# One product for gate and up, half of down in three float32r products, the last two blocks placed on chip

## The chip, the cores and the metric

The kernel runs on one core of a Trainium2 chip. The metric is the device time of one execution in microseconds (us), as the median of the runs.

## The reference

One layer of a diffusion backbone: 512 latent tokens of width 1024, 256 context tokens, one batch. First a token-mixing part (retention and gated DeltaNet in both directions, merged through one output projection), then a mixture of experts. The change touches the second part only. For each token a router takes 8 of 64 experts with weights, and

```
routed[t] = sum over the 8 experts e of  wts[t,e] * ( (silu(x[t] @ w_gate[e]) * (x[t] @ w_up[e])) @ w_down[e] )
shared[t] = (silu(x[t] @ w_sh_gate) * (x[t] @ w_sh_up)) @ w_sh_down
out[t]    = x1[t] + modulated rmsnorm(routed[t] + shared[t])
```

in float32, with `w_gate`, `w_up` 1024x256 and `w_down` 256x1024 for each expert. `x1` is the stream after the first part.

## The kernel before, in words

Everything up to about 700 us is the token-mixing part; it stays as it is. `phaseO` ends it: it writes `x1` into the output tensor (`self.out`), the normed tokens `h2` with the 64 routing weights beside them into DRAM (`h2d`, 1088 columns), and starts two sums in DRAM, `accd[0]` with the shared expert's result and `accd[1]` with zeros.

`phaseM` is the loop `for e in range(NE + 2)` (L1424), one block of up to 128 tokens for each expert (`NE` = 64), and one more, block 64, for an expert with more tokens than fit. For still more there is a loop on the chip (`tc.For_i`, L1459) behind it, whose count is read at run time. Iteration `e` works on three blocks at once: the products with gate and up of block `e`, the down product of block `e - 1`, and the transposed tokens of block `e + 2`.

* `prepare(e)` (L1284): GpSimd gathers the block's token rows from `h2d` with an indirect DMA into one of six buffers `xg`. The routing weight `W[e]` is a column of that buffer.
* `make(e, part)` / `turn` (L1232): TensorE transposes half of the tokens, ScalarE casts them to float32r (`h`), VectorE subtracts to get the remainder (`l`). A float32 product is then three float32r products, `h*h + h*l + l*h`: `mm3`, L111 to L113.
* `load(e, n)` (L1185): SyncE's queue loads one weight matrix of 1 MB; `n` is 0, 1, 2 for gate, up, down. Gate and up go into six buffers (`GU`, those called `w` and `wgu` in the profile), down into three (`DW`, called `wd`). For block 64 GpSimd does it, by an index.
* `convert(e, n)` (L1277): `conv` splits a gate or up matrix into cast (ScalarE, L1171) and remainder (VectorE, L1173), in two of seven buffers that all conversions share, and then issues the load of three blocks later into the buffer just read.
* `proj` (L1241): 8 x 3 products of 256 columns for gate, and the same for up, into two halves of one PSUM tile. `act` takes silu and the product, `turn_act` transposes it (`aT`).
* `down` (L1261): `aT` times the raw down weight as a plain float32 product, 2 halves of 512 columns x 2 parts of the contraction; in the trace each such product is two matmul instructions. The two halves are scaled by `W[e]` on VectorE and ScalarE into `y`, and GpSimd adds `y` to the sum in DRAM with an indirect DMA (L1272). Even and odd blocks go to different sums, the last four all to `accd[1]`.

After the loop, four tiles of 128 tokens are finished (L1473 on): `accd[1]` is loaded and added to `accd[0]` (loaded earlier), the norm's factor is formed with a power on GpSimd, the result is scaled, and `x1` is added, for two tiles by a DMA that adds in DRAM, for two on VectorE.

Each engine works through its instructions in order. The order is the scheduler's: it starts from the program's, lets instructions that it thinks are ready go ahead, and obeys `issue_after`. A wait at the head of an engine's queue holds up all behind it.

## Time and profile before

| | us |
|---|---|
| median of 3 runs (lowest, highest) | 1408.96 (1408.09, 1412.23) |
| the profiled execution | 1415.91 |
| its span, first to last instruction | 1414.1 |
| PE (TensorE matmul) busy | 1324.8 |
| DVE (VectorE) busy | 906.7 |
| ACT (ScalarE) busy | 653.4 |
| POOL (GpSimd) busy | 409.6 |
| HBM read, written | 326.59 MB, 48.31 MB |

The busy times are sums over the whole span and mix stages with different limits; what counts for this change is the loop over experts, from about 712 us, and the end behind it, from about 1381. Matmuls are pipelined, so a matmul's listed duration is longer than the step from one to the next. "Idle before, releaser" in a row is the engine's idle time ahead of these instructions and what ended it.

### The profile page before, as it was taken

Reading aid. Unit: us, or ns where it says so; the run is one execution under the profiler, and the core shown is the slowest. Engines: PE = TensorE matmul, PEld = TensorE weight load, DVE = VectorE, ACT = ScalarE, POOL = GpSimd, SP = SyncE. Lnnn points to the kernel's source line nnn. Section 1 sums busy time; section 2 is a strip of 40 time slices with the busy share of each in tenths; the row PEclk is TensorE's granted clock in tenths of the full one; section 3 lists DMA queues with packets and bytes.
Section 4 is the critical chain, followed back from the end, with each engine's and each line's share of the span. In section 5 each row is a group of like instructions: output and inputs, shape, how many; then the busy total and the mean of one; then the engine's idle time right before and its main releaser. Section 6 shows DMA issues by size and latency. Waiting matters only on the chain.

```text
span 1414.1 us, 20716 instructions
## 1 busy us (share of the span) xinstructions
PE 1324.8 (94%) x7848; PEld 1074.7 (76%) x7848; DVE 906.7 (64%) x1270; ACT 653.4 (46%) x926; POOL 409.6 (29%) x330
## 2 busy tenths in 40 slices
PE   6999988899999999999999999999999999999990
PEld 1678866798787777778888787878788888878770
DVE  5645796457676555547668666666666666666543
ACT  5533432553333222334355555555656565555531
POOL 0315544865321000003222222222222222224312
PEclk9899998999999999999999999999999999999995
DMA  7554411102316577575699999999999999999954
GB/s 275 181 141 117 121 56 35 52 16 74 88 49 179 178 214 223 152 259 195 249 386 349 352 370 345 373 351 364 362 366 361 368 364 361 367 364 338 326 183 127
DMA packets 137817, 340.51 MB, mean 241 GB/s; under 512 B 28218, under 2 KB 83038, under 8 KB 112756
## 3 DMA queue, kind: packets, MB, share of 16 engines
q1 hardware_dynamic: 110952, 289.46, 57.2%
q0 software_dynamic: 19584, 38.99, 10.9%
q10 hardware_dynamic: 7180, 10.72, 2.2%
q8 instruction: 63, 1.03, 0.3%
q14 instruction: 38, 0.31, 0.1%
HBM read 326.59 MB, written 48.31 MB: 265 GB/s over the span
## 4 chain that ended last, share of the span: by engine, by line
PE 43%; DMA 7%; issue 1%; ACT 1%; POOL 1%; DVE 0%; DVEq 0%; SPq 0%; ACTq 0%; POOLq 0%
PE cs L1267 13%; PE acc L111 7%; PE acc L113 7%; PE acc L112 7%; DMA w<-in_w_up_dram 4%; PE ci L1236 3%; DMA w<-in_w_gate_dram 2%; PE ci L1066 2%; PE acc L1078 1%; PE acc L1256 1%; DMA w<-acc 1%; POOL fr L127 0%; DMA acc<-y,slots 0%; DMA acc<-y,sl_i 0%; ACT wh L1171 0%
## 5 line engine op out<-in xcount | busy, mean ns | idle before, releaser
L111 PE MATMUL acc<-wh,xT 128*128 128x256 f32 x1040 | 302.2, 291 | 0.0
L113 PE MATMUL acc<-wh,xT 128*128 128x256 f32 x1040 | 291.0, 280 | 0.0
L112 PE MATMUL acc<-wl,xT 128*128 128x256 f32 x1040 | 290.6, 279 | 0.0
L1173 DVE TENSOR_TENSOR wl<-w,wh 128x2048 fp32r<-128x2048 f32 x88 | 201.5, 2291 | 76.2 <-PE acc L112 75.2
L1267 PE MATMUL cs<-wd,aT 128*128 128x512 f32 x520 | 234.6, 594 | 4.5 <-DMA wd<-in_w_down_dram 3.6
L1272 POOL DMA_INDIRECT acc<-y,slots x64 | 101.9, 1593 | 466.5 <-ACT y L1269 427.8
L1171 ACT CAST wh<-w 128x2048 fp32r<-128x2048 f32 x88 | 167.5, 1904 | 99.5 <-PE acc L113 70.2
L111 PEld LDWEIGHTS acc<-wh,xT 128*128 128x128 f32 x1040 | 196.6, 189 | 0.2 <-issue 0.2
L112 PEld LDWEIGHTS acc<-wl,xT 128*128 128x128 f32 x1040 | 196.1, 189 | 0.2 <-issue 0.2
L113 PEld LDWEIGHTS acc<-wh,xT 128*128 128x128 f32 x1040 | 195.5, 188 | 0.0
L1267 PEld LDWEIGHTS cs<-wd,aT 128*128 128x128 f32 x520 | 93.8, 190 | 99.0 <-issue 95.1
L1239 DVE TENSOR_TENSOR xT<-ci,xT 128x512 fp32r<-128x512 f32 x130 | 89.2, 687 | 96.5 <-ACT xT L1238 96.1
L100 ACT CAST wu<-raw 128x1024 fp32r<-128x1024 f32 (+1 forms) x73 | 75.1, 1036 | 104.6 <-DMA raw<-in_w_in_dram 68.0
L111 PE MATMUL acc<-hTx,wu 128*128 128x512 f32 (+1 forms) x296 | 119.6, 404 | 1.5 <-ACT wu L100 1.5
L113 PE MATMUL acc<-hTx,wu 128*128 128x512 f32 (+1 forms) x296 | 117.7, 398 | 1.5 <-DVE wu L107 1.5
L1173 DVE TENSOR_TENSOR wl<-wgu,wh 128x2048 fp32r<-128x2048 f32 x42 | 96.2, 2291 | 34.6 <-PE acc L112 34.4
L112 PE MATMUL acc<-hLx,wu 128*128 128x512 f32 (+1 forms) x296 | 117.1, 396 | 0.0
L107 DVE TENSOR_TENSOR wu<-raw,wu 128x1024 fp32r<-128x1024 f32 (+1 forms) x61 | 78.7, 1299 | 55.4 <-ACT wu L100 55.4
L1171 ACT CAST wh<-wgu 128x2048 fp32r<-128x2048 f32 x42 | 79.8, 1901 | 53.5 <-PE acc L113 35.5
L1236 PEld LDWEIGHTS ci<-ident,xg 128*128 128x128 f32 x520 | 72.5, 191 | 30.6 <-issue 30.2
L1228 POOL DMA_INDIRECT xg<-h2d,slots x64 | 75.5, 1180 | 35.6 <-issue 18.0
L1236 PE MATMUL ci<-ident,xg 128*128 128x128 f32 x520 | 78.7, 275 | 0.1
(493 smaller groups left out, 2374.3 us busy)
## 6 DMA issues: line engine op xcount, KB each, us to landing
wd<-in_w_down_dram SPq DMA_DIRECT2D x64, 1024.0 KB
w<-in_w_gate_dram SPq DMA_DIRECT2D x43, 1024.0 KB
w<-in_w_up_dram SPq DMA_DIRECT2D x43, 1024.0 KB
raw<-in_w_in_dram SPq DMA_DIRECT2D x56, 512.0 KB
wgu<-in_w_gate_dram SPq DMA_DIRECT2D x21, 1024.0 KB
wgu<-in_w_up_dram SPq DMA_DIRECT2D x21, 1024.0 KB
mraw<-in_w_mod_dram SPq DMA_DIRECT2D x32, 512.0 KB
wm<-in_w_mod_dram SPq DMA_DIRECT2D x16, 512.0 KB
```

The costliest lines, as they stand in the source:

```text
L100: nc.scalar.copy(dst, src)
L107: (self.nc.gpsimd if eng == "pool" else self.nc.vector).tensor_tensor(dst, src, hi.bitcast(F32), op=OP.subtract)
L111: mm(out, ah, bh, start=start, stop=False)
L112: mm(out, ah, bl, start=False, stop=False)
L113: mm(out, al, bh, start=False, stop=stop)
L1171: nc.scalar.copy(h[:, i:i + max(n, 1024)], w[:, i:i + max(n, 1024)])
L1173: eng(l[:, i:i + n], w[:, i:i + n], h[:, i:i + n].bitcast(F32), op=OP.subtract)
L1228: nc.gpsimd.indirect_dma_start(xg[:, :], None, self.h2d[:, :], bass.IndirectOffsetOnAxis(ap=ix, axis=0), bounds_check=511, oob_is_err=False)
L1236: nc.tensor.transpose(ps[:, k * 128:k * 128 + 128], xv[:, :, c * 4 + k], self.ident)
L1239: tt(l, ps, h.bitcast(F32), op=OP.subtract)
L1267: nc.tensor.matmul(ps, aT[:, m], wd[:, s], start=k == 0, stop=k == 1)
L1272: nc.gpsimd.indirect_dma_start(self.accd[acc][:, :], bass.IndirectOffsetOnAxis(ap=sx, axis=0), y[:, :], None, bounds_check=511, oob_is_err ...
```

## The change

* Gate and up of a block are converted into one pair of tiles, `GH[e % 2]` and `GL[e % 2]`, and `proj` takes both in one product of 512 columns (two pieces of 256). It runs in two parts, four of eight contraction steps ahead of `turn_act` and four behind it. ScalarE casts each matrix in two pieces of 1024 columns.
* Half of the down weight (the first 512 of 1024 columns) is split too, into `DP` (one buffer), and the activations into `aP`; this half of the down product is `mm3`, the other stays plain float32. `convert(e, 2)` stands at the end of iteration `e`.
* `xg` has three buffers in place of six, and the routing weight is copied out of it (`wcol`). One remainder tile lies where three of the six were. The first loads are in another order.
* The results of blocks 63 and 64 are not added in DRAM. `down_parts` leaves them on chip as cast and remainder, `places` writes one-hot matrices of the rows' tokens, and `finish` multiplies the two, so that a PSUM tile holds what they add to 128 tokens. The sums in DRAM are loaded earlier (`accd[1]` in iteration 63, `accd[0]` in 64), `x1` in iteration 62, all four tiles of it.
* `finish` stands in the program ahead of the loop for further blocks, and once more in its body.

```diff
+        GU = [wp.tile([128, 2048], F32, name=f"wgu{i}") for i in range(4)]
+        GH = [wp.tile([128, 2, 2048], F32R, name=f"gh{i}") for i in range(2)]
+        GL = [wp.tile([128, 2, 2048], F32R, name="gl0"), self.hxpool.tile([128, 2, 2048], F32R, name="gl1", tag="b1")]
+        DP = wp.tile([128, 2, 2, 512], F32R, name="wdp")
...
+        def convert(e, n):
+            if e > NE:
+                return
+            w = raw(e, n)
+            if n < 2:
+                h, l = GH[e % 2][:, n], GL[e % 2][:, n]
+                for i in (0, 1024):
+                    nc.scalar.copy(h[:, i:i + 1024], w[:, i:i + 1024])
+            else:
+                h, l, w = DP[:, 0], DP[:, 1], w.rearrange("p (k f) -> p k f", k=2)[:, :, 0:512]
+                nc.scalar.copy(h, w)
+            tt(l, w, h.bitcast(F32), op=OP.subtract)
+            if n < 2:
+                load(e + 3, n)
...
-        for e, n in ((0, 0), (0, 1), (1, 0), (0, 2), (1, 1), (2, 0), (1, 2), (2, 1), (2, 2)):
+        for e, n in ((0, 0), (0, 1), (1, 0), (1, 1), (0, 2), (1, 2), (2, 0), (2, 1), (2, 2)):
...
-        xg6, xg3 = q.tile([128, 3, 1088], F32, name="xg", bufs=1), self.hxpool.tile([128, 3, 1088], F32, name="xg", tag="b1")
-        xgs = [x[:, i] for x in (xg6, xg3) for i in range(3)]
+        xg3 = q.tile([128, 3, 1088], F32, name="xg", bufs=1)
+        xgs = [xg3[:, i] for i in range(3)]
...
-        def proj(out, x, w, first=True):
-            for k in range(8):
+        def proj(out, x, e, ks=range(8)):
+            o = out.rearrange("p (n f) -> p n f", n=2)
+            for k in ks:
                 s = slice(k * 256, k * 256 + 256)
-                self.mm3(out, x[0][:, k], x[1][:, k], w[0][:, s], w[1][:, s], k == 0, k == 7)
+                self.mm3(o, x[0][:, k], x[1][:, k], GH[e % 2][:, :, s], GL[e % 2][:, :, s], k == 0, k == 7)
...
-            aT = q.tile([128, 256], F32, name="aT")
+            aT, aP = q.tile([128, 256], F32, name="aT"), q.tile([128, 2, 256], F32R, name="aP", bufs=1)
+            nc.scalar.copy(aP[:, 0], ps[:, 0:256])
+            tt(aP[:, 1], ps[:, 0:256], aP[:, 0].bitcast(F32), op=OP.subtract)
             nc.scalar.copy(aT, ps[:, 0:256])
-            return aT
+            return aT, aP
+        def down_half(aT, wd, c):
+            ps = self.pc()
+            for k in range(2):
+                m = slice(k * 128, k * 128 + 128)
+                if c == 0:
+                    self.mm3(ps, aT[1][:, 0, m], aT[1][:, 1, m], DP[:, 0, k], DP[:, 1, k], k == 0, k == 1)
+                else:
+                    nc.tensor.matmul(ps, aT[0][:, m], wd[:, k * 1024 + 512:k * 1024 + 1024], start=k == 0, stop=k == 1)
+            return ps
...
+        def down_parts(aT, ws, wd, y):
+            for c in range(2):
+                ps = down_half(aT, wd, c)
+                h, l = y[:, c * 512:c * 512 + 512], y[:, 1024 + c * 512:1536 + c * 512]
+                nc.scalar.activation(h, ps, AF.Copy, scale=ws)
+                self.parted = nc.vector.scalar_tensor_tensor(l, ps, ws, h.bitcast(F32), op0=OP.mult, op1=OP.subtract)
+            return y
+        def places(oh, row):
+            at = q.tile([128, 4], F32, name="at", bufs=2)
+            for t in range(4):
+                ts(at[:, t:t + 1], row, -128.0 * t, None, op0=OP.add)
+                ts(oh[:, t], cst("r0"), at[:, t:t + 1], None, op0=OP.is_equal)
+        def finish(m, x1, blocks):
+            mg = [x[:, 0:1024] for x in xgs] + [self.rawp.tile([128, 1024], F32, name="mg", tag="raw")]
+            r = q.tile([128, 4], F32, name="fr")
+            PS = {}
+            def place(t, j):
+                oh, y = blocks[j]
+                for c in range(2):
+                    if j == 0:
+                        PS[t, c] = self.pc() if t == 3 else self.pi() if c else self.pa()
+                    for i in range(2):
+                        nc.tensor.matmul(PS[t, c], oh[:, t], y[:, i * 1024 + c * 512:i * 1024 + c * 512 + 512],
+                                         start=j == 0 and i == 0, stop=j == len(blocks) - 1 and i == 1)
+            for t in (0, 1):
+                place(t, 0)
+            for t in range(4):
+                if t > 1:
+                    place(t, 0)
+                for j in range(1, len(blocks)):
+                    place(t, j)
...
+            def add(t):
+                for c in range(2):
+                    s = slice(c * 512, c * 512 + 512)
+                    then(lambda: tt(m[t][:, s], PS[t, c], m[t][:, s], op=OP.add))
+                junk = q.tile([128, 1024], BF, name="xT", bufs=2)
+                nc.scalar.activation(junk, m[t], AF.Square, scale=D ** -0.5, accum_out=r[:, t:t + 1])
+                nc.scalar.activation(r[:, t:t + 1], r[:, t:t + 1], AF.Identity, bias=self.eps)
+                if t == 1:
+                    nc.gpsimd.tensor_tensor(mg[t], m[t], g2p, op=OP.mult)
+                nc.gpsimd.tensor_tensor(r[:, t:t + 1], r[:, t:t + 1], self.mhalf, op=OP.pow)
+            def scaled(t):
+                then(lambda: tt(mg[t], m[t], g2p, op=OP.mult))
+            def out(t, s, eng):
+                then(lambda: nc.vector.scalar_tensor_tensor(mg[t][:, s], mg[t][:, s], r[:, t:t + 1], x1[t][:, s], op0=OP.mult, op1=OP.add))
+                eng.dma_start(self.out[t * 128:t * 128 + 128, s], mg[t][:, s])
+            whole = slice(0, 1024)
+            add(0)
+            scaled(0)
+            add(1)
+            out(0, whole, nc.sync)
+            add(2)
+            scaled(2)
+            add(3)
+            out(1, whole, nc.scalar)
+            scaled(3)
+            out(2, whole, nc.sync)
+            out(3, slice(0, 512), nc.scalar)
+            out(3, slice(512, 1024), nc.sync)
...
+                if W[e] is None:
+                    W[e] = q.tile([128, 1], F32, name="wcol", bufs=4)
+                    nc.scalar.copy(W[e], XG[e][:, 1024 + e:1025 + e])
...
-                proj(pgu[:, 0:256], x(e), cv[e, 0])
+                proj(pgu, x(e), e, range(4))
...
-                proj(pgu[:, 256:512], x(e), cv[e, 1])
+                proj(pgu, x(e), e, range(4, 8))
...
+            if e > NE - 1:
+                Y.append(down_parts(aT, W[e - 1], raw(e - 1, 2), GH[(NE - 1) % 2][:, len(Y)]))
+            elif e > 0:
+                down(aT, SL[e - 1], W[e - 1], raw(e - 1, 2), (e - 1) % 2 if e < NE - 2 else 0)
+                load(e + 2, 2)
             if e > 0:
-                down(aT, SL[e - 1], W[e - 1], raw(e - 1, 2), 1 if e - 1 > NE - 4 else (e - 1) % 2)
-                load(e + 2, 2)
+                convert(e, 2)
...
+                x1 = halves(NE - 2)
                 for t in range(4):
-                    nc.sync.dma_start(m0[t], self.accd[0][t * 128:t * 128 + 128])
+                    nc.sync.dma_start(x1[t], self.out[t * 128:t * 128 + 128])
+            if e == NE - 1:
+                m1 = halves(NE)
+                for t in range(4):
+                    nc.sync.dma_start(m1[t], self.accd[1][t * 128:t * 128 + 128])
+            if e == NE:
+                m = halves(NE - 1)
+                for t in range(4):
+                    nc.sync.dma_start(m[t], self.accd[0][t * 128:t * 128 + 128])
+                with tc.issue_after(self.parted.ins):
+                    for t in range(2):
+                        tt(m[t], m[t], m1[t], op=OP.add)
                 for t in range(2, 4):
-                    nc.sync.dma_start(x1[t], self.out[t * 128:t * 128 + 128])
+                    nc.gpsimd.tensor_tensor(m[t], m[t], m1[t], op=OP.add)
+        finish(m, x1, list(zip(OH, Y)))
```

## Rows read from the trace of the kernel before

**Rows 1.** the page, busy tenths in 40 equal slices of the span.

```profile
PE   6999988899999999999999999999999999999990
...
DMA  7554411102316577575699999999999999999954
```

**Rows 2.** windows: PE, PEld, DVE, ACT, POOL busy (count), clock, DMA share, GB/s.

```profile
712.00:1256.00 544.00, 544.00 (x3554) 444.16 (x3554) 373.95 (x367) 320.93 (x374) 138.69 (x106) 1.00 1.00 363
1012.13:1022.36 10.23, 10.23 (x69) 8.32 (x68) 6.90 (x7) 6.00 (x7) 2.63 (x2) 1.00 0.97 357
...
1300.00:1325.00 25.00, 24.40 (x150) 18.97 (x150) 16.75 (x15) 12.63 (x15) 9.27 (x6) 1.00 0.99 345
```

**Rows 3.** the chain of waits, loop and end: start, us, what it went through.

```profile
1002.41 3.44 PE cs L1267 x8
...
1012.62 3.44 PE cs L1267 x8
...
1259.27 25.89 DMA w<-in_w_gate_dram
...
1383.19 4.62 DMA acc<-y,sl_i
1389.12 8.80 DMA w<-acc
```

**Rows 4.** ACT's timeline: start, us, instruction, idle before and what ended it.

```profile
716.52 1.91 ACT L1171 CAST wh<-wgu 128x2048 fp32r<-128x2048 f32 x1 [2.49 <-DMA wgu<-in_w_gate_dram]
...
1264.17 1.91 ACT L1171 CAST wh<-wgu 128x2048 fp32r<-128x2048 f32 x1 [2.09 <-PE acc L113]
...
1270.04 1.90 ACT L1171 CAST wh<-wgu 128x2048 fp32r<-128x2048 f32 x1 [2.44 <-DMA wgu<-in_w_up_dram]
...
1340.19 1.93 ACT L1171 CAST wh<-w 128x2048 fp32r<-128x2048 f32 x1
...
1348.38 1.91 ACT L1171 CAST wh<-w 128x2048 fp32r<-128x2048 f32 x1 [5.71 <-DMA w<-in_w_up_dram]
...
1381.49 0.69 ACT L1269 ACTIVATE y<-cs,sl_w 128x512 f32<-128x512 f32 x1 [3.79 <-PE cs L1267]
```

**Rows 5.** the timeline of SyncE's DMA issues, loop start.

```profile
707.33 0.33 SPq L1193 DMA_DIRECT2D wgu<-in_w_gate_dram  x1
```

**Rows 6.** PE's timeline, 512-column steps (151 us) and 256-column steps (1006 us).

```profile
151.08 0.40 PE L111 MATMUL acc<-hTx,wu 128*128 128x512 f32 x1
...
153.83 0.39 PE L111 MATMUL acc<-hTx,wu 128*128 128x512 f32 x1
...
1006.36 0.28 PE L113 MATMUL acc<-wh,xT 128*128 128x256 f32 x1
...
1008.81 0.28 PE L113 MATMUL acc<-wh,xT 128*128 128x256 f32 x1
```

**Rows 7.** groups by line and form from 550 us: busy, mean ns, idle before.

```profile
L1173 DVE TENSOR_TENSOR wl<-w,wh 128x2048 fp32r<-128x2048 f32 x88 | 201.5, 2291 | 76.2 <-PE acc L112 75.2 <-ACT aT L1258 0.8
...
L1271 DVE TENSOR_SCALAR y<-cs,xg 128x512 f32<-128x512 f32 x64 | 47.7, 745 | 3.6 <-PE cs L1267 3.6
...
L1258 ACT COPY aT<-acc 128x256 f32<-128x256 f32 x65 | 23.7, 365 | 4.8 <-PE acc L1256 4.8
L107 DVE TENSOR_TENSOR wu<-raw,wu 128x1024 fp32r<-128x1024 f32 x17 | 23.4, 1384 | 11.9 <-ACT wu L100 11.9
...
L100 ACT CAST wu<-raw 128x1024 fp32r<-128x1024 f32 x17 | 17.6, 1049 | 32.5 <-DMA raw<-in_w_in_dram 19.3 <-PE ci L113 6.1 <-DMA raw<-in_w_o_dram 3.5
...
L1116 POOL TENSOR_TENSOR h<-mix,mrow 128x512 f32<-128x512 f32 x4 | 7.1, 1787 | 5.8 <-DVE mix L1112 2.9 <-PE ci L1019 1.5 <-issue 1.5
```

**Rows 8.** the timeline of the end.

```profile
1397.94 1.22 DVE L1478 TENSOR_TENSOR w<-w,wgu 128x1024 f32<-128x1024 f32 x1 [2.50 <-DMA w<-acc]
...
1400.83 1.29 DVE L1484 SCALAR_TENSOR_TENSOR w<-w,fr,g2p 128x1024 f32<-128x1024 f32 x1 [0.23 <-POOL fr L127]
...
1408.58 0.34 ACTq L1489 DMA_DIRECT2D out_dram<-w  x1
```

More of the change, by code (lines that the diff above doesn't have):

```diff
@@ L1263, in down @@
             for c in range(2):
-                ps = self.pc()
-                for k in range(2):
-                    s, m = slice(k * 1024 + c * 512, k * 1024 + c * 512 + 512), slice(k * 128, k * 128 + 128)
-                    nc.tensor.matmul(ps, aT[:, m], wd[:, s], start=k == 0, stop=k == 1)
+                ps = down_half(aT, wd, c)
                 if c:
@@ L1273, in down @@
                                          bounds_check=511, oob_is_err=False, compute_op=OP.add)
[L1275 to L1280 removed]
+        def down_parts(aT, ws, wd, y):
+            for c in range(2):
+                ps = down_half(aT, wd, c)
+                h, l = y[:, c * 512:c * 512 + 512], y[:, 1024 + c * 512:1536 + c * 512]
+                nc.scalar.activation(h, ps, AF.Copy, scale=ws)
+                self.parted = nc.vector.scalar_tensor_tensor(l, ps, ws, h.bitcast(F32), op0=OP.mult, op1=OP.subtract)
+            return y
@@ new lines, in places, with then @@
+        def places(oh, row):
[22 more added lines that the diff above has]
+                    place(t, j)
+            last = [None]
+            def then(f):
+                if last[0] is None:
+                    last[0] = f()
+                else:
+                    with tc.issue_after(last[0].ins):
+                        last[0] = f()
+            def add(t):
+                for c in range(2):
+                    s = slice(c * 512, c * 512 + 512)
+                    then(lambda: tt(m[t][:, s], PS[t, c], m[t][:, s], op=OP.add))
+                self.d("moe", m[t], t)
+                junk = q.tile([128, 1024], BF, name="xT", bufs=2)
[22 more added lines that the diff above has]
+            out(3, slice(512, 1024), nc.sync)
@@ L1310, in phaseM @@
             convert(1, 0)
+            convert(0, 2)
         for e in range(2):
@@ L1420, in extra_list @@
             slot_of(pv, 1, sl)
+            self.xrow = sl[0]
             return wi, sl[1], sl[2]
         x = lambda e: [XT[e][:, h] for h in range(2)]
+        halves = lambda e: [raw(e, n)[:, i * 1024:i * 1024 + 1024] for n in range(2) for i in range(2)]
+        Y = []
         for e in range(NE + 2):
+            if e == NE:
+                OH = GL[(NE - 1) % 2][:, 0, 0:1024].rearrange("p (b t n) -> p b t n", b=2, t=4)
+                OH = [OH[:, 0], OH[:, 1]]
+                row = q.tile([128, 1], F32, name="row", bufs=1)
+                nc.vector.tensor_copy(row, slots[:, NE - 1:NE])
+                places(OH[0], row)
+                places(OH[1], self.xrow)
             if e == 3:
@@ L1465, in phaseM @@
                 load(NE, n, wi)
[L1466 removed]
+                convert(NE, n)
             pgu = self.pa()
[L1468 to L1489 removed]
+            proj(pgu, [xT[:, h] for h in range(2)], NE)
+            aT = turn_act(act(pgu[:, 0:256], pgu[:, 256:512]))
+            y = down_parts(aT, ws, raw(NE, 2), GH[(NE - 1) % 2][:, 0])
+            finish(m, x1, [(OH[0], y)])
         self.pes.close()
```

56 lines of the change are left out of this document (13 added, 43 removed).

## The prediction

> **What bounds the kernel now.** Read four views, in this order. First the slices of the page: from the 21st of 40 slices on, that is from about 707 us, PE stands at 9 in every slice but the last, and the DMA engines in every one but the last two [rows 1]. So the second half of the run, the loop over 64 experts, is not bound by one thing that can be read off: two resources are full at once. Second the windows: from 712 to 1256 us PE is busy for 544.00 of 544 us, and the DMA share is 1.00 at 363 GB/s; one block shows DVE at 6.90 and ACT at 6.00 of 10.23 us, so those two have a third of their time free [rows 2]. Third the chain of waits, which tells which of the two full ones is really limiting: up to 1256 us it goes through PE alone, with one block every 1012.62 - 1002.41 = 10.21 us, and from 1259 us on it goes through loads of weights (25.89 us from issue to the wait's end) [rows 3]. Fourth ACT's timeline says the same from the side that waits: after the loop has started up it waits for no weight load until 1270.04, and then gate conversions come at 1264.17 and, seven blocks later, at 1340.19, so 76.02 / 7 = 10.86 us a block [rows 4].
>
> So PE sets the loop's pace for (1270.04 - 716.52) / 10.21 = 54 blocks, and all this time the loads lose ground. How much: a gate load issued at 707.33 ended ACT's wait at 716.52, 9.2 us later, with others beside it [rows 4, 5]; at 1259 a load takes 25.9, which is all that the three blocks of prefetch give. 16.7 us of lead were eaten in 54 blocks, 0.31 a block. DMA's own pace is then 10.21 + 0.31 = 10.5 us as a mean over the loop, and 10.86 where it is seen alone. This is the number on which the prediction turns.
>
> **The profiled execution and the median.** The profiled execution took 1415.91 us, with a span of 1414.1 us, 1.8 us beside it. That is 6.95 us over the median of 1408.96. The stretch in which DMA leads, 1264 to 1340, costs 76.02 - 7 x 10.21 = 4.6 us over PE's pace; I estimate that most of the 7 us lies there, and that the runs without a profile still have some lead left at the end. Differences below are taken off the median.
>
> **The change part by part.**
>
> Gate and up as one product. Removed: 48 matmuls of 256 columns a block; added: 24 of 512. Starts are what counts, not durations: 21 steps of the first kind take 1008.81 - 1006.36 = 2.45 us, 0.1167 each; 12 steps of the second 153.83 - 151.08 = 2.75 us, 0.229 each [rows 6]. 48 x 0.1167 = 5.60, 24 x 0.229 = 5.50: 0.10 us saved a block. The bound below nothing: at 0.2334, twice the short one, nothing is saved.
>
> Half of down as three float32r products. Eight float32 steps take 3.44 us, 0.43 each [rows 3]. Four of them, 1.72, give way to 2 x 3 x 0.229 = 1.37: 0.35 us saved. Together PE needs 10.21 - 0.45 = 9.76 us a block, and 64 blocks could give 29 us.
>
> What pays for it. ACT and DVE convert half of each down weight and the activations: DVE +1.38 (the 128x1024 remainder) + 0.42 (128x256; ACT takes 0.37 for that shape, and I take a little more); ACT +1.05 (128x1024) + 0.37 + 0.37 for the copy of the weights' column (at most; it is one column wide), and 0.4 because gate and up are now cast in two pieces of 1.05 in place of one of 1.905 [rows 7]. DVE comes to 8.7, ACT to 8.2, both under 9.76. That cover is thin for DVE: it runs in order, and today it stands still for PE 76 us in 88 gate and up conversions [rows 7]. These waits come from seven shared buffers; the change gives each block its own pair, so I take them as gone.
>
> Does PE's gain arrive? Each block still loads 3 x 1024 KB, gathers its tokens and adds its result into DRAM; nothing of DMA's work goes but the last two blocks' additions. At 9.76 the lead of 16.7 us is used up after 16.7 / (10.5 - 9.76) = 23 blocks, and the rest runs at DMA's pace. The last up load then lands where it lands now (conversion at 1348.38 [rows 4]), less what the DMA engines idle today. Bounds: 0, if they idle nowhere; 29, if they follow PE all the way. I take 6: some 3 us from the first 100 us, where a load came in 9.2 us and the engines so had moments without work, and about half of the 7 us by which the median lies below the profiled run. It is nearer to 0, since the share is 1.00 from 712 on.
>
> [...]
>
> Buffers and queues. Gather buffers go from six to three; a gather is still issued in POOL's order behind the block's addition, and its buffer was last read a block earlier, so no wait is added. The down load is now needed at the end of its block's predecessor and not in mid-block, some 6 us earlier; ACT, when it waits for it, holds up the token and gate casts queued behind. With loads already late this eats lead once, about 6 us of it, and is no cost per block while DMA is the pace. The first loads are reordered and the second pair of remainders lies where the shared expert's weights were; the loop starts after these are read in either version. I take nothing; the bounds are 3 us either way.
>
> The end. Today, from the up conversion at 1348.38 to the last scaled result at 1381.49 + 0.7 = 1382.2 it is 33.8 us, then 31.9 to the span's end: the additions of the last two blocks in turn (the second 4.62), the load of the sums (8.80 until the last), the norm, the output, whose last issue at 1408.58 is 5.5 before the end [rows 3, 4, 8]. After the change the last two blocks stay on chip: three blocks of PE work less 3 x 0.45 = 1.3 us; then the two parts of the result (0.7 + 0.75), two sums of 1.22 on DVE beside the placing products (32 x 0.229 = 7.3 us, of which only the first four, 0.9, stand before DVE's work), DVE's chain of 8 x 0.69 + 3 x 1.22 + 3 x 1.28 + 2 x 0.69 = 14.4 us, and 5.5 for the output: 1.4 + 2.4 + 14.4 + 5.5 = 23.7. (0.69 and 0.75 are the 128x512 forms on ACT and DVE, and I take 0.69 for DVE's shorter sums; 1.22 is the 128x1024 sum, 1.28 the scaled one [rows 4, 7, 8].) The gain is 31.9 - 23.7 + 1.3 = 9.5. POOL can take from it: it gets two sums and one product of 128x1024, about twice 1.79 us each [rows 7], in order ahead of the first power, which the first output waits for: 0 to 4 us. I take 0.5, so 9. The sums must have landed by then: the last addition into DRAM is now two blocks before the end, 13 us of PE work, against 4.62 + 8.80: just in time. The loop over further blocks, which now stands behind the output, isn't entered with this input: today the last addition lands at 1383.19 + 4.62 = 1387.81 and the piece of the load begins at 1389.12, so it costs at most 1.3 us, and I take nothing.
>
> Sum: 6 + 9 = 15 us; 1408.96 - 15 = 1394.
>
> **The rivals.**
>
> PE keeps its gain. For it: PE is 100% busy for 544 us, and 363 GB/s may not be the ceiling. Against it: the ground lost before 1256 and the waits after it at PE's present pace; at 9.76 DMA would have to move 3.71 / 9.76 = 380 GB/s. It gives 29 + 9: 1371.
>
> DMA gives nothing more. For it: share 1.00, and 345 GB/s is all that is moved in the stretch in which loads are waited for (3.71 MB / 345 = 10.75 us a block). Then the loop ends where it does and the end alone gains: 1400. [...]
>
> The conversions bind. DVE is in order: if its waits for others stay as they are (10.23 - 6.90 = 3.33 a block) and the added 1.80 goes on top, a block takes 12.0 us. It decides from the point at which more than 10.21 - 9.76 = 0.45 of the 1.80 isn't absorbed. Unlike a late load it has no lead to eat first: a block of 10.5 costs 64 x 0.29 = 19 us, less the 9 of the end: 1419. Against it: with each buffer pair free a block earlier, a conversion's wait for PE has no cause. The clock could join it, were PE to rest more; but with 24.40 of 25 busy it was granted 1.00 [rows 2].
>
> The end doesn't get shorter: POOL's 10.7 us of wide operations delay the powers, or the sums land late. Then 6 of the loop less 4: 1406.
>
> **How the numbers follow.** Forecast 0.47 (1394, its own range 1386 to 1402); DMA gives nothing 0.17; PE keeps its gain 0.18; conversions bind 0.11; the end no shorter 0.07. 0.3%, about what a measurement here can tell from no change, is 4.2 us: faster means under 1404.7. That is most of the first three, 0.81; same 0.08; slower 0.11. The range takes in the rival below and stops at the old time above: 1370 to 1408.
>
> **What would show it.** In the profile after: steps of 0.229 in the joint product and in half of down; windows with PE below 25 of 25 and DMA at 1.00 from some block between the 20th and 40th on; ACT waiting for weight loads in each block from there; 10.5 to 10.9 us between blocks; the last up load landing between 1335 and 1348; no addition into DRAM after the last two blocks, and 22 to 28 us from the last scaled result to the end. Wrong would be PE at 25 of 25 to the end at 9.8 a block, or DVE full with DMA below 0.95.

## The result, and the profile after

The changed kernel takes 1417.22 us (median of 7 runs, 1413.84 to 1420.52), the kernel before beside it 1408.31 (7 runs, 1403.31 to 1412.23): a ratio of 1.0055, 95% interval 1.0035 to 1.0076. It is slower, by half a percent, 23 us over the forecast and outside its range. The profiled execution took 1418.97 us with a span of 1417.2.

The page after, busy tenths in 40 slices, answers to [rows 1]. In the loop's slices, from the 21st on, PE reads 9 in all but the 33rd and the last: the page hides most of the time that PE stands, and the windows below show it.

```profile
PE   6998978899999999999899999999999989999993
...
DMA  8543411102236567556899999999999999999962
```

Windows of the loop after (columns as in [rows 2]), then PE's turns of the activations, one pair a block: those of blocks 0, 10, 29, 61 and 64.

```profile
725.00:1000.00 275.00, 275.00 (x1250) 211.39 (x1249) 237.59 (x276) 212.09 (x335) 76.96 (x56) 1.00 1.01 370
1100.00:1300.00 200.00, 184.76 (x799) 135.48 (x798) 150.78 (x147) 135.97 (x218) 54.95 (x37) 0.99 0.98 344
```
```profile
721.31 0.39 PE L1272 MATMUL acc<-ident,sg 128*128 128x128 f32 x2
820.03 0.39 PE L1272 MATMUL acc<-ident,sg 128*128 128x128 f32 x2
1005.53 0.39 PE L1272 MATMUL acc<-ident,sg 128*128 128x128 f32 x2
1352.19 0.39 PE L1272 MATMUL acc<-ident,sg 128*128 128x128 f32 x2
1377.40 0.40 PE L1272 MATMUL acc<-ident,sg 128*128 128x128 f32 x2
```

Up to block 29 a block takes (1005.53 - 820.03) / 19 = 9.76 us, the forecast to the hundredth. From there to block 61 it takes (1352.19 - 1005.53) / 32 = 10.83, and PE stands 15 of 200 us. What PE had gained is given back, and more.

ACT's timeline and SyncE's issues for the last up weights answer to [rows 4, 5].

```profile
1345.80 1.04 ACT L1191 CAST gh<-wgu 128x1024 fp32r<-128x1024 f32 x1 [1.85 <-DMA wgu<-in_w_up_dram]
```
```profile
1321.39 0.33 SPq L1207 DMA_DIRECT2D wgu<-in_w_up_dram  x1
```

To compare the two executions I count from the last of DVE's eight searches for the largest places (MAX8), which stands ahead of the changed work on the compute engines: at 693.41 us before, at 685.19 after. The profiled execution before came there late; in the other traces here it is between 683.6 and 690.9, with either loop.

```profile
693.41 0.43 DVE L1208 MAX8 left<-left 128x8 f32<-128x256 f32 x1
```
```profile
685.19 0.43 DVE L1222 MAX8 left<-left 128x8 f32<-128x256 f32 x1
```

| stretch, us | before | after |
|---|---|---|
| last search to the first turn of activations | 28.9 | 36.1 |
| last search to the cast of the last up weights | 655.0 | 660.6 |
| that cast to the last turn of activations (before at 1376.55) | 28.2 | 31.6 |
| last turn of activations to the span's end | 37.6 | 39.8 |

The last three rows give 5.6 + 3.4 + 2.2 = 11.2 us more; the medians differ by 8.9. The start's 7 us lie inside the second row. In the third row PE has less work after the change, and yet it grew: 26.7 to 28.2 us in the five traces of the old loop that waited for the last up weights, 31.6 to 34.0 in the eight of the new one. By the program the joint product needs the up weights at its start; before, up's products came second, half a block later.

The end, DVE's timeline (answers to [rows 8]), then PE's.

```profile
1382.00 1.22 DVE L1580 TENSOR_TENSOR wgu<-wgu,wgu 128x1024 f32<-128x1024 f32 x1 [2.57 <-DMA wgu<-acc]
1385.43 1.23 DVE L1580 TENSOR_TENSOR wgu<-wgu,wgu 128x1024 f32<-128x1024 f32 x1 [2.21 <-DMA wgu<-acc]
1386.58 0.42 DVE L1275 TENSOR_TENSOR aP<-acc,aP 128x256 fp32r<-128x256 f32 x1
...
1407.80 1.40 DVE L1365 SCALAR_TENSOR_TENSOR mg<-mg,fr,wgu 128x512 f32<-128x512 f32 x2
```
```profile
1387.05 0.80 PE L113 MATMUL cs<-wdp,aP 128*128 128x512 f32 x1 [6.30 <-DVE aP L1275]
```

The sums of the two accumulators stand in DVE's queue ahead of block 64's activations, because the order is tied to block 63's parts. DVE waits for their loads, and PE for DVE.

### The profile page after: what moved, and what is told of

Same layout as the page of the kernel before. It is cut to its first block, busy times and chain, and to the rows that moved or that the text cites. A ratio compares the mean times of both kernels' runs of the same rounds, so it can differ in the third digit from the quotient of the medians.

```text
span 1417.2 us, 18240 instructions
## 1 busy us (share of the span) xinstructions
PE 1313.7 (93%) x6450; PEld 1023.4 (72%) x6450; DVE 1004.3 (71%) x1423; ACT 757.8 (53%) x1256; POOL 420.0 (30%) x326
## 3 DMA queue, kind: packets, MB, share of 16 engines
q0 software_dynamic: 19008, 37.68, 10.5%
## 5 line engine op out<-in xcount | busy, mean ns | idle before, releaser
L1191 ACT CAST gh<-wgu 128x1024 fp32r<-128x1024 f32 x260 | 272.8, 1052 | 139.7 <-DMA wgu<-in_w_up_dram 54.6
L1195 DVE TENSOR_TENSOR gl<-wgu,gh 128x2048 fp32r<-128x2048 f32 x130 | 297.1, 2286 | 34.6 <-ACT gh L1191 30.2
L111 PE MATMUL acc<-gh,xT 128*128 128x512 f32 x520 | 216.5, 416 | 0.0
L113 PE MATMUL acc<-gh,xT 128*128 128x512 f32 x520 | 205.6, 395 | 0.0
L112 PE MATMUL acc<-gl,xT 128*128 128x512 f32 x520 | 204.1, 392 | 0.0
L1287 PE MATMUL cs<-wd,aT 128*128 128x512 f32 x260 | 126.6, 609 | 21.3 <-ACT aT L1276 21.1
L113 PEld LDWEIGHTS acc<-gh,xT 128*128 128x128 f32 x520 | 97.8, 188 | 23.3 <-issue 0.5
L111 PEld LDWEIGHTS acc<-gh,xT 128*128 128x128 f32 x520 | 99.0, 190 | 17.0 <-issue 0.7
L112 PEld LDWEIGHTS acc<-gl,xT 128*128 128x128 f32 x520 | 98.4, 189 | 16.7 <-issue 0.2
L1265 DVE TENSOR_TENSOR sg<-sg,acc 128x256 f32<-128x256 f32 x65 | 27.3, 420 | 97.7 <-ACT sg L1264 97.7
L1287 PEld LDWEIGHTS cs<-wd,aT 128*128 128x128 f32 x260 | 47.7, 191 | 66.6 <-issue 31.8
L1195 DVE TENSOR_TENSOR wdp<-wd,wdp 128x1024 fp32r<-128x1024 f32 x65 | 79.0, 1215 | 0.2 <-ACT wdp L1194 0.2
```

The source lines that it names most:

```text
L111: mm(out, ah, bh, start=start, stop=False)
L112: mm(out, ah, bl, start=False, stop=False)
L113: mm(out, al, bh, start=False, stop=stop)
L1191: nc.scalar.copy(h[:, i:i + 1024], w[:, i:i + 1024])
L1195: tt(l, w, h.bitcast(F32), op=OP.subtract)
L1287: nc.tensor.matmul(ps, aT[0][:, m], wd[:, k * 1024 + 512:k * 1024 + 1024], start=k == 0, stop=k == 1)
```

## The experiments

The runs were taken in groups, with the kernel before beside each group, at 1408.20 to 1409.97 us. A difference of 4 us or less between groups is weak evidence by itself.

**The order at the end, and the loop alone.**

e1, the sums moved out of the loop and so behind block 64's work:

```diff
-                with tc.issue_after(self.parted.ins):
...
+        with tc.issue_after(self.parted.ins):
+            for t in range(2):
+                tt(m[t], m[t], m1[t], op=OP.add)
...
```

> The changed kernel with one edit: the four sums of the two accumulators stand behind block 64's parts of the result in DVE's and POOL's order, no longer behind block 63's. Theory of the order (mine): in the changed kernel's trace DVE waited in its queue for the load of the sums and only then made the remainder of block 64's activations (at 1386.58 us), and PE stood 6.30 us for it and went on at half its clock; with the sums behind it, this remainder comes some 7 us earlier and PE keeps its clock: 8 to 10 us less than the changed kernel, 1407 to 1410 us. Rival: the end waits for the landing of the sums or for the last loads, whatever stands first in DVE's queue: 1415 to 1418 us.

Measured: 1418.37 us (8 runs), ratio 1.0062 [1.0034, 1.0090]. My first theory fell. DVE's stall is gone in the trace, but the sums now follow the last parts, and the loop ended later in this execution:

```profile
1384.97 0.41 DVE L1275 TENSOR_TENSOR aP<-acc,aP 128x256 fp32r<-128x256 f32 x1
...
1389.30 0.75 DVE L1307 SCALAR_TENSOR_TENSOR gh<-cs,sl_w,gh 128x512 fp32r<-128x512 f32 x1 [0.97 <-ACT gh L1306]
1389.97 2.35 DVE L1581 TENSOR_TENSOR wgu<-wgu,wgu 128x1024 f32<-128x1024 f32 x2
```

From the last turn of activations (1383.0 here) to the end it is 35.3 us instead of 39.8. The times show nothing of it.

e2, the new loop with the old end (the old lines from `m0 = ...` to the output put back, all blocks through `down`):

> The new loop (joint gate and up product, half of down as three products) with the end of the kernel before (all blocks added into DRAM, the loop over further blocks ahead of the norm). Theory that the end lost the time: the loop alone gains 2 to 3 us, as the last up conversion came 2.6 us earlier in the trace, so 1405 to 1410 us, and the old end is cheaper than the new one by about 8 us. Rival that the loop itself loses (more work on ACT and DVE between the last loads and the last products): 1415 us or more, as much as the changed kernel. If the loop kept PE's gain of 0.45 us a block it would be near 1380 us.

Measured: 1420.68 us (4 runs), ratio 1.0102 [1.0058, 1.0145]. The rival holds: the old end does not bring the time back. In its trace the last turn of activations comes 694.3 us behind the last search (before 683.1), and from there to the end it is 37.5 us (before 37.6).

**What the loads wait for.** e3, half of the down loads left out:

```diff
+                if n < 2 or e < 3 or e % 2 == 0:
                     nc.sync.dma_start(t, a[NAMES3[n]][0, e].rearrange("(p k) f -> p (k f)", p=128))
```

> As the first kernel of this group, but of the blocks from the fourth on each second one leaves out the load of its down weight (its product uses what lies in the buffer). Everything else is issued as before: PE's, ACT's and DVE's work is the same. Theory that the loads set the pace in the second half of the loop: half a MB of 3.71 MB a block goes, blocks come every 9.76 us to the end instead of 10.83 in the last 32, some 30 us less than the first kernel: 1375 to 1382 us. Rival that conversions or POOL's order set it: within 3 us of the first kernel.

Measured: 1378.43 us (4 runs), and 9.76 us a block to the end. The loads set the pace, not conversions or POOL.

e4, the tokens spread over the partitions, their bytes unchanged. It rests on a supposition of mine that no trace shows: the rows give some of the 16 DMA engines more to move than others, and the fullest sets the pace. What the changed kernel's trace shows is that, from 1000 us on, half of the 16 increments of a weight load have come 6 to 7 us after its issue and the last 22 to 24 us after it (medians of each 100 us):

```diff
-        nc.vector.tensor_copy(both[0:64, 0:64], first[0:64])
-        nc.vector.tensor_copy(both[64:128, 64:128], first[64:128])
+        for i in (0, 64):
+            nc.vector.tensor_copy(both[i:i + 64, i:i + 64].rearrange("p (b q c) -> p b q c", q=8, c=4),
+                                  first[i:i + 64].rearrange("p (b c q) -> p b q c", q=8, c=4))
```

> As the first kernel of this group, but the tokens of a block are dealt to other partitions: a block's tokens (on average 32 of 64 places of each half of the partitions are taken) now fill places 0, 1, 2, ... of each half; here they go to places 0, 4, 8, ..., 28, 1, 5, ... and then to the second 32. The bytes stay the same. [...] So PE leads to the end: 1375 to 1385 us. Rival that all engines, or the memory, are full (DMA share 1.00 in the windows): within 3 us of the first kernel. [...]

Measured: 1376.73 us (4 runs), ratio 0.979 [0.9741, 0.9838]; 41.6 us under e1. A window of e4:

```profile
1000.00:1300.00 300.00, 300.00 (x1352) 231.09 (x1351) 254.31 (x247) 233.12 (x368) 86.25 (x63) 1.00 1.02 381
```

PE is full at 9.76 us a block, and the DMA engines move 381 GB/s where the changed kernel got 344 while PE waited for them. The DMA share reads 1.02 here and 0.98 there: a share near 1 said nothing about what more could be moved.

e18, the control:

```diff
+        for i in (0, 64):
+            for b in (0, 32):
+                nc.vector.tensor_copy(both[i:i + 64, i + b:i + b + 32], first[i:i + 64, 32 - b:64 - b])
```

> A control for the spreading: both repairs (1420.7 us), and the two 32-partition quarters of each half change places, so that a block's first 32 tokens of each half lie on places 32 to 63 and the others on 0 to 31. [...] Theory that the gain of 42 to 47 us of the spread kernels comes from even rows over the engines: no gain, 1417 to 1424 us. Rival that it comes from something else in where the rows lie (which partitions are written, neighbouring rows): 1400 us or less. [...]

Measured: 1416.53 us (12 runs, 1410.06 to 1421.70), ratio 1.0048 [1.0026, 1.0069], half a microsecond under the range of the theory. All rows moved, and nothing was gained. So the gain of e4 is not that of moving rows at all; it goes with how e4 deals them out. That e4 evens out what the engines have to move, that e18 does not, and that the fullest engine was the limit before is my explanation and is not shown: no trace names the engine of a transfer.

**The change where the loads are in time.** e5 is the kernel before, e6 the new loop with the old end, e7 the changed kernel, each with e4's edit.

> The kernel before with the tokens spread over the partitions, nothing else. Theory of the fullest DMA engine: its 9.6 us a block then lie under PE's 10.2, so PE leads to the end; the kernel before waited for loads only in its last blocks (turn of block 61's activations at 627.9 us behind that of block 0, where 61 x 10.20 = 622.2), and the loads of the end also come sooner: 3 to 8 us less than before, 1401 to 1406 us. Rival (the engines as a whole are full, and the spread kernel of the first group gained for another reason): no change, within 2 us of before. If the spreading by itself were worth what it was worth in the changed kernel, it would be 40 us less, 1369 us; the theory excludes that.

Measured: 1401.27 us (10 runs), ratio 0.9960 [0.9943, 0.9978], at the lower edge of the theory's range: before, PE led nearly to the end anyway. The 9.6 us a block of a fullest engine are shown by no run; in e5's trace PE is busy for all of the 300 us from 1000 to 1300, with 365 GB/s moved.

> New loop, old end, tokens spread: with the kernel of the first group that spread them under the new end it tells what the new end is worth, and with the spread kernel before what the new loop is worth, both where DMA is not the limit. Theory: PE's 0.45 us a block arrive, 61 x 0.44 = 27 us less than the spread kernel before: 1374 to 1380 us. Rival (the conversions on ACT and DVE or the order of the new loop cost time in the blocks by themselves): 1385 us or more.

Measured: 1384.14 us (4 runs), between the two. Its blocks take 9.82 us in place of 9.76, 4 us in all, for a reason that I have not found (e2, the same program with the rows as they were, has 9.82 too from block 10 to 29, so it is not the spreading); the rest against e4 is the old end, 60.6 us from the turn of block 61 against 58.0.

> The changed kernel as it was, with its sums ahead of block 64's work, and the tokens spread. Against the spread kernel with the late sums (1376.7 us) it tells what the order of the sums costs where the loop's end does not wander with the loads. Theory of the order: 4 to 7 us more, 1380 to 1384 us (39.8 us from the last turn of activations to the end against 35.3 with the late sums, in the two unspread traces). Rival (with the loads in time the sums land before DVE comes to them): within 1 us, 1376 to 1378 us.

Measured: 1378.21 us (4 runs, 1375.73 to 1378.98; e4's go from 1374.38 to 1385.31): no clear difference, and its trace's end is even shorter (32.0 us from the last turn, e4's 33.3). So the rival holds: with the loads in time the place of the sums costs nothing. That they have landed when DVE comes to them is its explanation, which these figures alone do not show.

So the change is worth 1401.27 - 1378.21 = 23 us where the rows are spread, against 24.5 for e4.

**The start.** ACT's timeline in the changed kernel, ahead of the loop:

```profile
688.63 0.38 ACT L1071 ACTIVATE shg<-ci 128x256 f32<-128x256 f32 x1 [3.43 <-PE ci L1068]
700.62 0.19 ACT L1403 COPY wcol<-xg 128x1 f32<-128x1 f32 x1 [11.61 <-DMA xg<-h2d,slots]
702.25 0.19 ACT L1403 COPY wcol<-xg 128x1 f32<-128x1 f32 x1 [1.43 <-DMA xg<-h2d,slots]
702.34 0.58 ACT L1081 COPY y<-acc 128x512 f32<-128x512 f32 x1
...
704.05 0.38 ACT L1071 ACTIVATE shg<-ci 128x256 f32<-128x256 f32 x1 [0.46 <-ACT y L1081]
```

The copy of the weights' column, 0.19 us long, waits for the first gather, and the shared expert's last activation is queued behind it; PE's first block waits for that. Moving the copy (e9) makes the first turn of activations come 5 us sooner, so this wait is most of the start's 7 us. e9, e10 (with e1's edit) and e11 (with e1's and e4's) put it behind the casts:

```diff
-                    nc.scalar.copy(W[e], XG[e][:, 1024 + e:1025 + e])
-            turn(XT[e], part, XG[e])
+            cast = turn(XT[e], part, XG[e])
+            if part == 1 and W[e] is None:
...
+                with tc.issue_after(cast.ins):
+                    nc.scalar.copy(W[e], XG[e][:, 1024 + e:1025 + e])
```

> The changed kernel with one edit: ACT's copy of a block's weight column is ordered behind the second cast of the same block's tokens, in place of ahead of the first. Theory (the start): in every trace with the new loop, from the last of DVE's eight searches for the largest to the first turn of activations it is 35.1 to 35.9 us, in the three with the old loop 28.5 to 28.8; in the changed kernel's trace the first of these copies, a 128x1 form, stands 11.61 us for a gather, with the shared expert's last casts and activation queued behind it on ACT. Moved, the loop starts 6 to 7 us earlier and, as the loads follow the loop's conversions, all behind it moves along: 1409 to 1412 us. Rival (where loads set the pace the loop ends when they end, whenever PE starts): 1415 to 1418 us, as the changed kernel.

Measured: 1419.69 us (6 runs), ratio 1.0086 [1.0061, 1.0111]. In its trace the first turn comes 30.8 us behind the last search (715.52 - 684.72) and not 36.1, and the last turn 694.3 us behind it (after: 692.2). The gain at the start is gone by the end: the rival was right in kind, 2 us over its range.

```profile
715.52 0.39 PE L1273 MATMUL acc<-ident,sg 128*128 128x128 f32 x2
...
1378.97 0.40 PE L1273 MATMUL acc<-ident,sg 128*128 128x128 f32 x2
```
```profile
684.72 0.43 DVE L1222 MAX8 left<-left 128x8 f32<-128x256 f32 x1
```

> Both repairs in the changed kernel: the weight column's copy behind the casts, and the sums behind block 64's work. The start is then worth 6 to 7 us as in the run before; the traces say that the late sums shorten the end by 4.7 us (39.8 to 35.3 from the last turn of activations), the times said nothing (1418.4 against 1417.2). Theory that the end's 4.7 us are real and were covered by the loop's spread: 1404 to 1408 us. Rival that in a loop led by the loads the end's order is worth nothing: 1409 to 1412 us, as the run before. Either way no clear gain over the kernel before: the loop's 29 us of PE time are not there while the fullest DMA engine sets the pace.

Measured: 1420.67 us (6 runs), ratio 1.0093 [1.0069, 1.0117]: both of my ranges missed. In this kernel, whose loads lead, neither repair nor both brought a gain.

> Both repairs and the tokens spread over the partitions. With the spread kernel with late sums at 1376.7 us and the start 6 to 7 us shorter: 1369 to 1372 us. Rival that the start's 7 us are used up by the loop waiting for its first loads instead: 1375 to 1378 us.

Measured: 1373.47 us (6 runs, 1371.32 to 1379.50), ratio 0.9762 [0.9734, 0.9791], the fastest of all and between the two ranges. Where PE leads, some 3 us of the start arrive (from the last search to the last turn of activations 652.2 us, e4's 656.7).

e12, without the products for half of down (and without their casts):

> As the kernel before this, but without the second part of the change: down's first half is again two float32 products, and the casts and remainders of half the down weights and of the activations are left out; gate and up stay one product. It tells the two gains of PE apart where the loads are in time. By the prediction's terms 0.10 us a block come from the joint product and 0.35 from down's half: 61 x 0.35 = 21 us more than the kernel before this, 1390 to 1393 us, with blocks of 10.1 us. Rival that the joint product carries the most: under 1380 us.

Measured: 1395.39 us (5 runs), 2 us over the range, and 10.09 us a block. The joint product brings 10.20 - 10.09 = 0.11 us a block (10.20 is e5's), down's half 10.09 - 9.76 = 0.33.

**Why the loop got slower, and not only no faster.** e8, three gather buffers in the kernel before (`ng[0] % 3`; the weights' column then comes from a later block's rows):

> The kernel before with three gather buffers in use in place of six, nothing else. It asks why the new loop, where DMA sets its pace, ends 3 to 5 us behind the old one in the traces. Theory that the gathers, which now wait for a buffer and queue on the fullest engine behind the weights, come too late: 3 to 8 us more than before, 1412 to 1418 us. Rival, that a gather is issued in POOL's order behind the block's addition anyway (so the prediction): within 2 us of before.

Measured: 1408.49 us (10 runs), ratio 1.0002 [0.9981, 1.0023]: nothing.

e13, the old loop with less PE work (`for k in range(7)` in `proj`):

> The kernel before with one of the eight pieces of the sum left out of the gate and of the up product (so the result is not the reference's): 6 steps of 0.1167 us less, 9.5 us of PE work a block in place of 10.2, with the same order, buffers, loads and conversions. It asks whether a loop led by the fullest DMA engine is slower by itself. Theory A, the fullest engine sets the end and a faster PE neither helps nor harms: within 3 us of before, 1405 to 1411 us, and the new loop's 10 us from the last search to the last turn of activations (692 to 694 against 682 to 683) come from its own order or buffers. Theory B, once PE waits for the loads a block costs more than the engine alone would need: 1413 to 1420 us.

Measured: 1398.78 us (6 runs), ratio 0.9919 [0.9900, 0.9939]. Neither theory: the old loop, led by its loads from about block 27 on, gains 11 us from a faster PE (1409.60 for the kernel before in this group).

e14, the new loop with more PE work:

```diff
+                if k in (1, 5):
+                    nc.tensor.matmul(o, x[1][:, k], GL[e % 2][:, :, s], start=False, stop=False)
```

> The changed kernel with both repairs (weight column's copy, late sums: 1420.7 us) and two matmuls of 512 columns more in each block, remainder by remainder, which the sum leaves out otherwise: 2 x 0.229 us, PE back at 10.2 us a block, all else as it was. Theory A (the new loop's own order or buffers cost the time): no gain, 1418 to 1424 us. Theory B (being led by the loads costs the time): a slower PE makes it faster, 1405 to 1412 us, as the kernel before less the 2 to 4 us of the end.

Measured: 1423.90 us (6 runs), ratio 1.0097 [1.0080, 1.0114]. With PE at the old pace the new loop is as slow as with the new one. So the new loop's own order, conversions or buffers cost the time, and not the pace of PE.

e15, down's conversion half a block later:

```diff
-            convert(0, 2)
...
                 aT = turn_act(SG[e - 1])
+                convert(e - 1, 2)
...
-            if e > 0:
-                convert(e, 2)
```

> The changed kernel with both repairs, and the conversion of half a down weight put half a block later, behind the turn of its own block's activations; the down load is needed that much later. Theory that needing the down weights earlier costs time in the loop that the loads lead (the prediction took it as lead eaten once, about 6 us): 1412 to 1416 us. Rival that it costs nothing as long as the fullest engine always has loads queued: within 2 us of 1420.7 us.

Measured: 1416.86 us (7 runs, 1413.56 to 1418.94; e10's go from 1419.07 to 1424.40): 3.8 us less, 0.9 over the range of the theory and outside that of the rival. It does not settle the matter. e18, which differs from e10 in the rows' places alone and keeps the down weights' early need, came to 1416.53 as well. In the traces e15's last turn of activations comes 688.3 us behind the last search, e10's and e18's 692.4. But from the turn of block 0 to that of block 61 it takes 634.6 us against 635.8 and 636.4: most of the 4 us lies ahead of the loop, where a conversion went, and behind block 61. No cost per block is shown.

e16 (e13 with three gather buffers) and e17 (e13 with five weight buffers; its two main places):

```diff
-        raw = lambda e, n: DW[e % 3] if n == 2 else GU[(2 * e + n) % 6]
+        raw = lambda e, n: DW[e % 3] if n == 2 else GU[(2 * e + n) % 5]
...
-                load(e + 3, n)
+                load(e + 2 + n, 1 - n)
```

> The old loop with the faster PE (1398.8 us; a piece of the gate and up sums left out) and three gather buffers in use in place of six, so that the weights' column is taken from a later block's rows. The new loop has three. Where PE led (the run of the kernel before with three) they made no difference; here the loads lead. Theory that the gathers' buffers cost the new loop its 10 us: 1404 to 1410 us. Rival that they don't matter here either: 1397 to 1401 us.

Measured: 1400.52 us (9 runs): the gather buffers are not it.

> The old loop with the faster PE (1398.8 us; a piece of the gate and up sums left out) and five buffers in place of six for the gate and up weights, each load issued one conversion later; so 2.5 blocks of them are under way or held in place of 3. Theory of the reach: the new loop gives its loads 22 to 24 us from issue to the need, the old one with the fast PE 26 to 29, because the joint product wants the up remainder, and down's conversion the down weights, half a block earlier; the fullest engine is not the same in each block, and a shorter reach evens out less. Five buffers take some 5 us off the reach, as the new loop does: 1404 to 1412 us. Rival that an engine that always has loads queued doesn't care how many: 1397 to 1401 us.

Measured: 1404.49 us (12 runs), ratio 0.9968 [0.9950, 0.9985]; 5.7 us over e13, and 4.0 over e16, which ran beside it. The last up weights, issue and cast, in e13 and then in e17, and PE's turns of blocks 0, 29 and 61 in the same order:

```profile
1306.02 0.33 SPq L1193 DMA_DIRECT2D w<-in_w_up_dram  x1
```
```profile
1335.58 1.91 ACT L1171 CAST wh<-w 128x2048 fp32r<-128x2048 f32 x1 [5.03 <-DMA w<-in_w_up_dram]
```
```profile
1318.76 0.33 SPq L1193 DMA_DIRECT2D w<-in_w_up_dram  x1
```
```profile
1339.60 1.90 ACT L1171 CAST wh<-w 128x2048 fp32r<-128x2048 f32 x1 [2.35 <-DMA w<-in_w_up_dram]
```
```profile
715.76 0.51 PE L1256 MATMUL acc<-ident,sg 128*128 128x128 f32 x2 [1.20 <-DVE sg L1249]
993.79 0.41 PE L1256 MATMUL acc<-ident,sg 128*128 128x128 f32 x2
1337.04 0.41 PE L1256 MATMUL acc<-ident,sg 128*128 128x128 f32 x2
```
```profile
714.97 0.50 PE L1256 MATMUL acc<-ident,sg 128*128 128x128 f32 x2 [1.57 <-DVE sg L1249]
997.51 0.41 PE L1256 MATMUL acc<-ident,sg 128*128 128x128 f32 x2
1343.45 0.41 PE L1256 MATMUL acc<-ident,sg 128*128 128x128 f32 x2
```

The reach, from issue to cast, falls here from 29.6 to 20.8 us, and the cast comes 653.9 us behind the last search instead of 648.7. After the change the reach is 24.4 [1345.80 - 1321.39] and the cast comes at 660.6. So in the old loop a shorter reach costs time; that the fullest engine changes from block to block, the theory's reason, is not shown. Most of it is lost once: up to block 29 e17 takes 282.5 us and e13 278.0, since the blocks get longer from the 17th on in place of the 26th; in the 32 blocks behind it is 345.9 against 343.3.

## Why the prediction was wrong

- **PE's pace.** Right: 9.76 us a block, 0.11 and 0.33 for the two parts against 0.10 and 0.35. The steps in the joint product are 0.227 apart at the loop's start (six from 716.04 to 717.40); from block 12 to 28 they are 0.238 as a mean, and the old product's 0.121, so both were taken 3 to 4% too short. The conversions were absorbed, as forecast.
- **When the lead is used up.** About right: 23 blocks forecast, 29 in the trace, then 10.83 a block against 10.5 to 10.86.
- **"I take 6" (the loop's end).** This step failed. The last up weights came 5.6 us later from the last search on, not 6 earlier: some 12 us of the miss. (In the two traces' own times the cast came 2.6 us earlier, inside the window that the prediction names as a sign; but the profiled run before had come to the last search 8.2 us later.) Two things are in it. I read the share of 1.00 in [rows 2] as a pace that DMA can't exceed; with the same bytes at other places it moves 381 GB/s and PE doesn't wait for it (e4), so the pace hangs on where the rows lie. That alone would have left a gain: in the old order with a faster PE the last up weights come at 648.7 in place of 655.0, and 11 us are gained (e13). The second is the sentence on buffers and queues. It says that the earlier need of the down weights eats lead once, about 6 us, and "is no cost per block while DMA is the pace", and the sum then puts it at nothing. But lead is not free: in the old loop a shorter reach costs 5.7 us, most of it once (e17). A cost per block is not shown, and how much of the new loop's loss comes from the down weights is open, since e15 does not tell.
- **The up weights' earlier need.** The prediction does not ask when the joint product needs the up weights. From the cast of the last of them to the last turn it took 31.6 us, where by its sum it would be 28.2 - 1.3 = 26.9. That the half block of the program's order is the cause is argued and not shown: it can't be moved without undoing the product, and no run tests it from the other side.
- **"Half of the 7 us" by which the profiled run lies over the median.** Wrong: that execution came to the last search 2.5 to 9.9 us later than the other traces did, ahead of the loop; it says nothing of the loads.
- **"I take nothing; the bounds are 3 us" (start).** Wrong in size: 7 us. I priced the copy of the weights' column at 0.37 us of ACT and did not ask what it waits for, nor what stands behind it. Moved, it brings nothing while the loads lead (e9) and some 3 us where PE leads (e11).
- **The end, 9 us.** This step failed too, and by more: from the cast of the last up weights to the span's end it is 71.4 us, before 65.7, so 5.7 more in place of 9 less. From the last scaled result on the forecast seems right: 1417.2 - (1392.58 + 0.69) = 23.9 us against 23.7. That is luck in part: the 23.7 hold two sums of 1.22 that DVE had made earlier here, and where it makes them in this stretch (e1) it takes 29.0. What failed ahead of it is "the sums must have landed by then ... just in time". They came 6 us too late for DVE's place in the order, and from the cast of the last up weights to the last scaled result it took 47.5 us, before 33.8. With the late sums of e1 the new end is worth 37.6 - 35.3 = 2.3 us from the last turn on, not 9. The late sums alone were not what made the kernel slower (e1, e2).
- **The rivals.** Nearest was "DMA gives nothing more". Its 1400 fell with the end's 9 us and the later loads. The 3.71 MB a block that two rivals divide are 363 GB/s x 10.21 us [rows 2, 3]; e4 has 381 x 9.76 = 3.72, at the 380 GB/s that "PE keeps its gain" asked for. "Conversions bind" had the right side and the wrong mechanism: DVE was free 49 of 200 us in the second window. The sum of "The end doesn't get shorter" is 1407, not 1406.

Open: why the last up weights come later in the new loop, beyond what e17 shows of a shorter reach; the 4 us of e6's longer blocks; why e1's shorter end in the trace shows in no time (its last turn came 696.7 us behind the last search, after the change 692.2, so the two traces end alike); the loads of the residual input, which now stand ahead of the last down weights in SyncE's order, were not tried.

## What to carry to other kernels

When two resources are full at once, first ask of the busier-looking one whether it could move more: here the DMA engines moved 344 GB/s at a share of 0.98 in the changed kernel and 381 at 1.02 in e4, and dealing the same rows to other partitions was worth 42 us in the changed kernel (e4 against e1), and 7 in the kernel before, where PE led (e5). What a faster engine is worth beside loads that lead depends on the order around it: 11 us in the old loop (e13), next to nothing in the new one (e14 against e10). Lead that an order eats once is a term of the sum, even where the loads set the pace (5.7 us in e17). A small instruction is priced by its wait and by what is queued behind it, not by its length: the copy of 0.19 us waited 11.61 us, and most of the start's 7 us came of it.

## What the hardware showed that I had not expected

- A DMA share of 0.98 to 1.02 went with 344, 361, 370 and 381 GB/s in the windows of this case. By the packets of the traces before and after, the 8 KB transfers of the weights take 0.309 us as a median in the windows of 344, 361 and 370, over three quarters of them to the nanosecond (78 to 79%).
- By the trace's records half of the 16 increments of a 1 MB load come within 5 to 10 us of its issue, the last only 20 to 30 us after it, where the loads lead (after, e13); with the rows spread the last come after 7 to 17 us (e4).
- PE's granted clock at the changed kernel's end (windows, columns as in [rows 2]): 1.00 while PE was full, and as a mean 0.62 in the 13 us of which PE then stood half, with 0.50 from 1384 to 1393. The next float32r product is listed with 0.80 us in place of 0.39 (the row of 1387.05 above), and the next three start 0.43 us apart in place of 0.23.

```profile
1368.00:1380.00 12.00, 12.00 (x50) 8.79 (x49) 4.89 (x7) 4.49 (x9) 1.55 (x1) 1.00 0.49 121
1380.00:1393.00 13.00, 6.70 (x14) 3.66 (x13) 3.53 (x4) 1.48 (x3) 4.66 (x2) 0.62 0.43 153
```
